# A fused LoRA kernel whose first load of 128 rows is issued as four transfers of 16, 16, 32 and 64 rows

## The chip, the cores and the metric

The kernel runs on one core of one Trainium2 chip. The metric is the device time of one execution in microseconds. Where a median is given, it is that of the runs shown beside it. All times in the profile are microseconds from the first instruction of the profiled execution.

## The reference

```python
def setup_inputs():
    batch, seq, d_model, r = 16, 512, 768, 16
    # x [16, 512, 768], A [768, 16], B [16, 768], float32; scale = 0.5

def reference(x, A, B, scale):
    lora = np.matmul(np.matmul(x, A), B)
    return (x + scale * lora).astype(np.float32)
```

The input x and the output have 8192 tokens of 768 float32 values, 25.17 MB each. A and B are 48 KB each.

## The kernel before

The 8192 tokens are 64 tiles of 128 tokens. `PARTS = [8, 8, 16, 16, 16]` groups them into five parts of x; in a part with S tiles partition p holds S tokens that follow one another in memory, so one partition reads or writes one contiguous run (`memory`, line 96). With S = 8 this run is 8 x 768 x 4 = 24,576 bytes. `x_all` holds 48 of the 64 tiles; the last part takes the room of the first two once these have been stored.

Seven loads (`LOADS`, line 106) and five stores (`STORES`, line 130) move x. All of them, and the small loads of A and B, are issued on SP's queue, in this order: the first load (line 140, ahead of the section in which the engines run their own programs), three loads of A as soon as POOL has cleared `a_rows` (line 163), B as soon as `b_rows` is cleared (line 167), four more loads of x (line 169), the first two stores (line 178, after the second group's first products), a load after each of these two stores has landed (lines 181 and 183), two stores, and the last store behind the section (line 361). Each load k has a semaphore of its own, `s_load[k]`, which counts 16 for a transfer.

The work goes in eight groups of eight tiles (`GROUP = 8`). For one group:

- ACT and POOL cast four tiles each to float16 into `xn` (`narrowed`, line 195, the copy on line 203). The first use of a load waits for its `s_load` (line 200).
- DVE transposes `xn` to `xt` in blocks of 32 (line 260); in the first group it does so in two halves (lines 271 to 274).
- PE multiplies by the block-diagonal weights `w_bd` into `y_ps`, 24 matmuls (line 290), ACT scales these into `y_bd` (line 245), and PE multiplies by `b_mm` into `lora` (line 311), two tiles at a time.
- DVE adds `lora` to x in place (line 265); when a part is finished, SP stores it.

DVE works one group behind the transposes: it transposes group g + 1 and then adds group g. PE's loop (line 333) interleaves in the same way. At the start, PE also waits for the weights: A is loaded, transposed by DVE (line 253) and spread by POOL (lines 220 to 229); B is loaded, cast by ACT (line 236), picked apart by PE (line 324) and cast again (line 238).

The first load is marked so that the planner adds no dependencies of its own to it (`no_tile_sem_insts`, and the group "first", which a no-op on POOL closes as a fence on line 144). The waits on `s_load[0]` in `narrowed` are the only ones for its data.

Of the kernel before, what the change touches and what calls it, by code (L numbers as in the profile page):

```python
# [28 lines left out]
def kernel(  # L29
# [8 lines left out]
    nc = tc.nc  # L38
    fp32 = mybir.dt.float32
    P = 128  # L40
# [3 lines left out]
    x2 = x.flatten_outer_dims()  # L44
# [38 lines left out]
    def sem(name):  # L83
        sems.append(nc.alloc_semaphore(name))
        return sems[-1]
# [10 lines left out]
    def memory(t2, i, s, n):  # L96
        S = PARTS[i]
        return t2[ds(parts[i], S * P), :].rearrange("(p s) d -> p s d", s=S)[:, ds(s, n), :]

    def held(i, s, n):  # L100
        return tiles(where.index((i, s)), n)

    def tiles(t, n):
        return x_all[:, ds(t % ROOM, n), :]

    LOADS = [
        (0, 0, 8), (1, 0, 8), (2, 0, 8), (2, 8, 8), (3, 0, 16), (4, 0, 8), (4, 8, 8)
    ]
    s_load = [sem(f"s_load{k}") for k in range(len(LOADS))]

    def load_of(t):
        i, s = where[t]
        return next(k for k, ld in enumerate(LOADS) if ld[0] == i and ld[1] <= s < ld[1] + ld[2])
# [20 lines left out]
    def load(k):  # L134
        ld = LOADS[k]
        return nc.sync.dma_start(out=held(*ld), in_=memory(x2, *ld)).then_inc(s_load[k], 16)

    first = load(0)  # L140
    tc.no_tile_sem_insts.add(first.ins.name)
    tc.add_to_no_dep_group("first", first.ins)
    begun = nc.gpsimd.nop()
    tc.declare_fence(begun.ins, group="first")

# [49 lines left out]
    def narrowed(e, copy, g, first, n=SUB):  # L195
        t = g * GROUP + first
        for k in dict.fromkeys(load_of(t + k) for k in range(n)):
            if (e, k) not in here:
                here.add((e, k))
                e.wait_ge(s_load[k], 16)  # L200
        if g:
            e.wait_ge(s_taken, g)
        ins = copy(out=xn[:, ds(first, n), :], in_=tiles(t, n))  # L203

        ins.then_inc(s_narrow if g else s_second if first else s_first, 1)

    def on_gpsimd(e):
        e.memset(a_rows[0:Q], 0.0).then_inc(s_ready, 1)  # L208
        e.memset(b_rows, 0.0).then_inc(s_brows, 1)  # L209
        e.memset(pick, 0.0).then_inc(s_pick, 1)  # L210
        e.memset(w_bd.rearrange("p c k m -> p (c k m)").bitcast(fp32), 0.0)  # L211
        e.memset(y_bd.rearrange("p s m -> p (s m)").bitcast(fp32), 0.0).then_inc(s_ready, 1)  # L212
        e.wait_ge(s_pick, 1)
        e.affine_select(  # L214
            out=pick, in_=pick, compare_op=mybir.AluOpType.not_equal, fill=1.0, base=0,
            pattern=[[0, NQ], [-APART, Q]], channel_multiplier=1,
        ).then_inc(s_pick, 1)
        narrowed(e, e.tensor_copy, 0, 0)
        e.wait_ge(s_ready, 3)
        e.tensor_copy(  # L220
            out=w_one.rearrange("i (c e) k r -> i c e (k r)", c=SETS),
            in_=a_t[0:Q].rearrange("i k r (e c) -> i c e (k r)", c=SET)[:, 0:SETS, 0:SET, :],
        ).then_inc(s_w, 1)
        e.wait_ge(s_w, 1)
        for b in range(NQ):
            e.tensor_copy(  # L226
                out=w_bd[ds(b * Q, Q), :, :, ds(b * Q, R)], in_=w_one
            ).then_inc(s_w, 1)
            e.wait_ge(s_w, b + 2)
        for g in range(1, NG):  # L230
            narrowed(e, e.tensor_copy, g, SUB)

    def on_scalar(e):
        narrowed(e, e.copy, 0, SUB)
        e.wait_ge(s_b, 16)
        e.copy(out=b_half, in_=b_rows).then_inc(s_bh, 1)  # L236
        e.wait_ge(s_bp, 1)
        e.copy(out=b_mm, in_=lora[0][:, 0, :]).then_inc(s_bm, 1)  # L238
        for g in range(NG):
            if g + 1 < NG:  # L240
                narrowed(e, e.copy, g + 1, 0)
            e.wait_ge(s_y, g + 1)
            for b in range(NQ):
                q = ds(b * Q, Q)
                last = e.mul(out=y_bd[q, :, q], in_=y_ps[q, :, :], mul=sc)  # L245
                if b == 0 and g + 1 < NG:

                    last.then_inc(s_narrow, 1)
            last.then_inc(s_spread, 1)
# [151 lines left out]
```

## Time and profile before

| | |
|---|---|
| median of 3 runs | 123.59 us (123.36 to 123.59) |
| profiled execution | 123.44 us |
| its span, first to last instruction | 121.7 us |
| DMA moved | 50.43 MB on one queue, mean 415 GB/s |
| DVE busy | 81.7 us (67% of the span) |
| PE, ACT, POOL busy | 50.0, 36.8, 28.8 us |
| granted TensorE clock, mean | 0.922 |

The page cuts the span into 40 slices of 3.04 us: a digit is the busy share in tenths. The row "DMA" is the mean busy share of the core's 16 DMA engines, "GB/s" what they moved. In a view of windows each row is a stretch of time, and its last columns are the granted clock, the DMA share and GB/s. In the chain of waits each row is a start, a duration and the engine or transfer that the end waited for. In the timeline each row is a start, a duration, the engine (SPq is SP's queue, and its time is that of the issue, not of the transfer), the line and the operation, and in brackets how long the engine was idle before, and what released it.

### The profile page before, as it was taken

Reading aid. Unit: us, or ns where it says so; the run is one execution under the profiler, and the core shown is the slowest. Engines: PE = TensorE matmul, PEld = TensorE weight load, DVE = VectorE, ACT = ScalarE, POOL = GpSimd, SP = SyncE. Lnnn points to the kernel's source line nnn. Section 1 sums busy time; section 2 is a strip of 40 time slices with the busy share of each in tenths; the row PEclk is TensorE's granted clock in tenths of the full one; section 3 lists DMA queues with packets and bytes.
Section 4 is the critical chain, followed back from the end, with each engine's and each line's share of the span. In section 5 each row is a group of like instructions: output and inputs, shape, how many; then the busy total and the mean of one; then the engine's idle time right before and its main releaser. Section 6 shows DMA issues by size and latency. Waiting matters only on the chain.

```text
span 121.7 us, 887 instructions
## 1 busy us (share of the span) xinstructions
PE 50.0 (41%) x322; PEld 29.2 (24%) x322; DVE 81.7 (67%) x42; ACT 36.8 (30%) x43; POOL 28.8 (24%) x23
## 2 busy tenths in 40 slices
PE   0000139477457547746745734774674420000000
PEld 0000016244233324424423312442442110000000
DVE  0002870699999999999999979999995991000000
ACT  4003728535408402835340193733004000000000
POOL 7603958035008002605300180620000000000000
PEclk9999999999999999999999999999999998555555
DMA  4999999999998897999999999998899899899890
GB/s 129 388 461 412 436 452 404 436 452 404 452 517 388 388 517 323 444 444 404 444 428 412 452 428 469 404 517 388 388 517 404 388 501 436 388 469 469 372 452 0
DMA packets 1784, 50.43 MB, mean 415 GB/s; under 512 B 220, under 2 KB 220, under 8 KB 248
## 3 DMA queue, kind: packets, MB, share of 16 engines
q1 hardware_dynamic: 1784, 50.43, 96.7%
HBM read 25.26 MB, written 25.17 MB: 414 GB/s over the span
## 4 chain that ended last, share of the span: by engine, by line
DVE 36%; DMA 29%; PE 9%; ACT 5%; POOL 2%; issue 1%
DVE x_sb L265 22%; DMA x_sb<-in_x_dram 20%; DVE xt L260 14%; DMA out_dram<-x_sb 9%; PE ps_yt L290 6%; PE lora_ps L311 3%; ACT y_bd L245 3%; POOL xn L203 2%; ACT xn L203 2%
## 5 line engine op out<-in xcount | busy, mean ns | idle before, releaser
L265 DVE TENSOR_TENSOR x_sb<-x_sb,lora_ps 128x1536 f32<-128x1536 f32 x32 | 53.7, 1734 | 1.4 <-PE lora_ps L311 1.4
L311 PE MATMUL lora_ps<-b_mm,y_bd 128*128 128x512 f16 (+1 forms) x128 | 25.0, 328 | 22.9 <-ACT y_bd L245 14.6
L203 POOL CAST xn<-x_sb 128x3072 f16<-128x3072 f32 x8 | 22.0, 2748 | 49.7 <-DMA x_sb<-in_x_dram 32.2
L203 ACT CAST xn<-x_sb 128x3072 f16<-128x3072 f32 x8 | 22.0, 2752 | 35.9 <-DMA x_sb<-in_x_dram 26.2
L260 DVE STREAM_TRANSPOSE xt<-xn 128x3072 f32<-128x3072 f32 (+1 forms) x9 | 27.0, 3007 | 6.3 <-ACT y_bd L245 5.8
L290 PE MATMUL ps_yt<-xt,w_bd 128*128 128x256 f16 x192 | 25.4, 283 | 10.8 <-DVE xt L260 10.8
L290 PEld LDWEIGHTS ps_yt<-xt,w_bd 128*128 128x128 f16 x192 | 18.6, 99 | 18.4 <-issue 14.0
L311 PEld LDWEIGHTS lora_ps<-b_mm,y_bd 128*128 128x128 f16 x128 | 10.5, 97 | 35.7 <-ACT y_bd L245 16.8
L245 ACT ACTIVATE y_bd<-ps_yt 32x256 f16<-32x256 f32 x32 | 12.0, 375 | 18.5 <-PE ps_yt L290 18.1
L253 DVE STREAM_TRANSPOSE a_t<-a_rows 32x1024 f32<-32x1024 f32 x1 | 2.0, 1964 | 11.4 <-DMA a_rows<-in_A_dram 11.4
L324 PE MATMUL lora_ps<-b_half,pick 128*128 128x512 f16 (+1 forms) x2 | 0.8, 500 | 14.7 <-ACT b_half L236 14.7
L324 PEld LDWEIGHTS lora_ps<-b_half,pick 128*128 128x128 f16 x2 | 0.1, 105 | 14.7 <-issue 14.7
L226 POOL COPY w_bd<-w_one 32x384 f16<-32x384 f16 x4 | 2.0, 501 | 0.2
L203 ACT ACT_TABLE_LOAD x1 | 1.3, 1283 | 1.0 <-POOLq L147 1.0
L211 POOL MEMSET w_bd<- 128x1536 f32 x1 | 1.4, 1372 | 0.0
L238 ACT CAST b_mm<-lora_ps 128x768 f16<-128x768 f32 x1 | 0.8, 799 | 1.0 <-PE lora_ps L324 1.0
L208 POOL MEMSET a_rows<- 32x1024 f32 x1 | 0.9, 942 | 0.6 <-POOLq L147 0.6
L220 POOL CAST w_one<-a_t 32x384 f16<-32x384 f32 x1 | 0.8, 843 | 0.0
L236 ACT CAST b_half<-b_rows 128x768 f16<-128x768 f32 x1 | 0.8, 826 | 0.0
L209 POOL MEMSET b_rows<- 128x768 f32 x1 | 0.7, 727 | 0.0
L212 POOL MEMSET y_bd<- 128x512 f32 x1 | 0.5, 515 | 0.0
L214 POOL TENSOR_SCALAR_AFFINE_SELECT pick<-pick 128x128 f16<-128x128 f16 x1 | 0.3, 300 | 0.0
(5 smaller groups left out, 0.6 us busy)
## 6 DMA issues: line engine op xcount, KB each, us to landing
x_sb<-in_x_dram SPq DMA_DIRECT2D x6, 3072.0 KB, 14.5
out_dram<-x_sb SPq DMA_DIRECT2D x3, 6144.0 KB, 19.3
x_sb<-in_x_dram SPq DMA_DIRECT2D x1, 6144.0 KB, 41.5
out_dram<-x_sb SPq DMA_DIRECT2D x2, 3072.0 KB, 14.2
a_rows<-in_A_dram SPq DMA_DIRECT2D x3, 16.0 KB
b_rows<-in_B_dram SPq DMA_DIRECT2D x1, 48.0 KB, 7.5
```

What stands on the lines that cost most here:

```text
L203: ins = copy(out=xn[:, ds(first, n), :], in_=tiles(t, n))
L208: e.memset(a_rows[0:Q], 0.0).then_inc(s_ready, 1)
L211: e.memset(w_bd.rearrange("p c k m -> p (c k m)").bitcast(fp32), 0.0)
L220: e.tensor_copy(out=w_one.rearrange("i (c e) k r -> i c e (k r)", c=SETS), in_=a_t[0:Q].rearrange("i k r (e c) -> i c e (k r)", c=SET)[:, ...
L226: e.tensor_copy(out=w_bd[ds(b * Q, Q), :, :, ds(b * Q, R)], in_=w_one).then_inc(s_w, 1)
L245: last = e.mul(out=y_bd[q, :, q], in_=y_ps[q, :, :], mul=sc)
L253: e.transpose(out=a_t[0:Q].rearrange("i k r c -> i (k r) c"), in_=a_rows[0:Q].rearrange("c (i k r) -> c (k r) i", k=2, r=R),).then_inc(s_r ...
L260: return e.transpose(out=ts[0], in_=ts[1])
L265: ins = e.tensor_tensor(out=xs, in0=xs, in1=lora[p % 2], op=mybir.AluOpType.add)
L290: mm = e.matmul(y_ps, w_bd[:, c, k, :], xv[:, :, c, :, k], start=(m == 0), stop=(m == MMS - 1),)
L311: mms.append(e.matmul(t[:, k, ds(n0, w)], y_bd[:, 2 * p + k, :], b_mm[:, ds(n0, w)], start=True, stop=True,))
L324: last = e.matmul(lora[0][:, 0, ds(n0, w)], pick.rearrange("p b r -> p (b r)"), b_half[:, ds(n0, w)], start=True, stop=True,)
```

## The change

The single issue of the first load is replaced by four, on the same queue and the same semaphore. `to[p:P:step]` takes every `step`-th partition from `p` on: partitions 0, 8, ..., 120 (16 rows), then 4, 12, ..., 124 (16 rows), then 2, 6, ..., 126 (32 rows), then the odd ones (64 rows). The four together move the same 128 rows, each row from and to the same place. The wait for load 0 is raised from 16 to 64. All other loads, stores and instructions stay as they are, on every engine, and in the same order.

```diff
-    first = load(0)
-    tc.no_tile_sem_insts.add(first.ins.name)
-    tc.add_to_no_dep_group("first", first.ins)
+    PIECES = [(0, 8), (4, 8), (2, 4), (1, 2)]
+    to, of = held(*LOADS[0]), memory(x2, *LOADS[0])
+    for p, step in PIECES:
+        piece = nc.sync.dma_start(out=to[p:P:step], in_=of[p:P:step]).then_inc(s_load[0], 16)
+        tc.no_tile_sem_insts.add(piece.ins.name)
+        tc.add_to_no_dep_group("first", piece.ins)
     begun = nc.gpsimd.nop()
     tc.declare_fence(begun.ins, group="first")
...
-                e.wait_ge(s_load[k], 16)
+                e.wait_ge(s_load[k], 16 if k else 16 * len(PIECES))
```

## The prediction

> **What bounds the kernel now.** I read the page's slices and queue rows first, then the chain of waits in order of time, then windows around the first load.
>
> ```profile
> PE 50.0 (41%) x322; PEld 29.2 (24%) x322; DVE 81.7 (67%) x42; ACT 36.8 (30%) x43; POOL 28.8 (24%) x23
> ...
> DMA  4999999999998897999999999998899899899890
> ...
> DMA packets 1784, 50.43 MB, mean 415 GB/s; under 512 B 220, under 2 KB 220, under 8 KB 248
> ...
> q1 hardware_dynamic: 1784, 50.43, 96.7%
> ```
>
> The DMA engines are full in nearly every slice but the first and the last, and DVE, the busiest compute engine, has 67%. So the time is a start, 50.43 MB at the full rate, and an end. All packets of 8 KB or more are 1784 - 248 = 1536 = 12 x 128: each of the seven loads and five stores of x moves one packet per partition, 24,576 bytes in the first load.
>
> ```profile
> 4.00:9.00 5.00, 0.00 (x0) 0.00 (x0) 0.00 (x0) 0.00 (x0) 0.91 (x3) 1.00 1.01 433
> 32.00:44.00 12.00, 7.15 (x48) 4.25 (x48) 12.00 (x7) 5.06 (x8) 2.75 (x1) 1.00 1.01 434
> 100.00:118.00 18.00, 0.00 (x0) 0.00 (x0) 0.85 (x1) 0.00 (x0) 0.00 (x0) 0.58 1.00 434
> ```
>
> The last two columns are the DMA share and GB/s. Loads alone (4 to 9 and 32 to 44 us) and stores alone (100 to 118) run at the same 433 to 434 GB/s with a share of 1.00 to 1.01. That is 433 / 16 = 27.1 GB/s for one of 16 engines, and 24,576 B / 27.1 GB/s = 0.91 us for one row. The first load is 8 rows per engine, 3.146 MB / 433 = 7.26 us.
>
> ```profile
> 0.74 10.35 DMA x_sb<-in_x_dram
> 11.09 0.05 issue
> 11.14 2.75 POOL xn L203
> ...
> 44.30 10.73 DMA out_dram<-x_sb
> 55.04 0.02 issue
> 55.05 14.55 DMA x_sb<-in_x_dram
> ```
>
> The chain begins with the load that is changed: issued at 0.74, landed 10.35 us later, which is 3.09 us more than 7.26. Whatever moves its end moves both the DMA queue behind it and the compute chain from 11.14 to the first store at 44.30, by about the same amount; the end follows one for one.
>
> **The start of the load.** The view of the DMA queue for 1 to 4 us, in 40 slices of 0.075 us (bytes are put down at the start of a packet):
>
> ```profile
> DMA  0000000000990999009797070070000999990709
> GB/s 0 0 0 0 0 0 0 0 0 0 983 655 0 655 328 328 0 0 328 328 655 328 0 328 0 0 328 0 0 0 0 655 655 983 655 655 0 328 0 655
> DMA packets 30, 0.74 MB, mean 246 GB/s; under 512 B 0, under 2 KB 0, under 8 KB 0
> ```
>
> A slice of 328 GB/s is one row begun (24,576 B / 0.075 us). Three begin at 1.75 us, and counting on, the sixteenth begins in the slice at 2.95; the next row begins only at 3.33, 1.58 us after the first three although a row takes 0.91. So the engines begin over 1.2 us, and the early ones are slow at first. Of the 0.74 MB begun by 4.00, half a row per engine (0.20 MB) is still to come: 0.54 MB done, which at 433 GB/s is a full flow begun at 4.00 - 1.25 = 2.75 us.
>
> **The change part by part.** *The engine's share of bytes* stays: 16, 16, 32 and 64 rows give each engine 1, 1, 2 and 4 rows if each piece spreads over all 16, the same eight. Each piece adds a completion on every engine, three more; in the next view 42 packets under 512 B pass with no fall of the rate, so nothing is taken for them.
>
> *Three more issues on SP.* From the timeline:
>
> ```profile
> 0.74 0.38 SPq L136 DMA_DIRECT2D x_sb<-in_x_dram  x1
> ...
> 1.06 0.94 POOL L208 MEMSET a_rows<- 32x1024 f32 x1 [0.62 <-POOLq L147]
> ...
> 2.03 2.01 SPq L163 DMA_DIRECT2D a_rows<-in_A_dram  x3
> ...
> 4.09 0.54 SPq L167 DMA_DIRECT2D b_rows<-in_B_dram  x1
> ...
> 4.68 2.07 SPq L136 DMA_DIRECT2D x_sb<-in_x_dram  x4
> ```
>
> One issue costs 0.38 us here, up to 2.01 / 3 = 0.67 later. Four pieces end at 0.74 + 4 x 0.38 = 2.3 to 0.74 + 4 x 0.67 = 3.4 instead of 1.12. The loads of A wait for a memset on POOL till 2.0 anyway, so they move from 2.03 by 0.3 to 1.4 us, and B and the four loads of x behind them end by 6.75 + 1.4 = 8.15. All of these queue behind the first load, whose 7.26 us from 2.75 last to 10.0: hidden with 1.8 us to spare. If that cover were gone, it would cost up to 1.4 us. Nor does the queue run dry between pieces: a piece comes every 0.38 to 0.67 us and keeps an engine busy for at least 0.91.
>
> *The start.* Sixteen rows instead of 128 have to be handed out before every engine has work. What this brings isn't in the trace: at best all engines flow fully from 1.75, a gain of 2.75 - 1.75 = 1.0 us; at worst the early slowness belongs to the first access and nothing is gained. Nothing is nearer to one end, so I take half, 0.5.
>
> *Which rows move together.* This decides the sign. The trace has the constant 27.1 GB/s per engine for 128-row transfers alone. It may be the limit of the engine, or of the part of SBUF that the row goes to, several partitions sharing one part. In the first case the pieces run at full rate: cost 0. In the second, a 128-row transfer runs undisturbed only because its rows are laid out so that no two engines go to one part at once. The pieces take partitions 0, 8, 16, ..., then 4, 12, ...: at one time all engines take rows of one kind, every second group of four partitions is left alone, and if the engines' numbers follow the rows, two engines share each part in every step: half rate, a cost of one more 7.26 us. What the trace has of narrow strided transfers is A and B (4 and 16 rows of 3 or 4 KB each):
>
> ```profile
> DMA packets 84, 0.46 MB, mean 464 GB/s; under 512 B 42, under 2 KB 42, under 8 KB 69
> ```
>
> From 9.7 to 10.7 us the 69 - 42 = 27 small data packets pass with no fall (464 GB/s). It speaks for the first case, but 27 packets of 4 KB are 0.1 MB, too short to fill whatever buffers lie between. Equal rates for reading and for writing HBM say that the limit is in the engine or on SBUF's side, and no more. I take the second case: the only shape shown at full rate is the one the change gives up, and the bursts against it are too small to count. From 7.26 something comes off: if two partners are d apart, the later is still in the old part for d while the earlier has moved on, and the rows make six stretches in one part (1, 1, 1, 1, 2, 2 rows), so 6d. With 1.2 us of spread cut to an eighth (16 rows for 128), d is about 0.1: 0.6 off. Ends: d = 0 (7.26), and d = 0.45, half a row (7.26 - 2.7 = 4.6).
>
> [...]
>
> **The sum.** The profiled execution took 123.44 us, 1.7 outside its span of 121.7; the median of the runs shown is 123.59, 0.15 above. Cost 7.26 - 0.6 for sharing, gain 0.5 at the start: +6.2, so 123.44 + 6.2 = 129.6.
>
> What is late next: the first store's issue moves from 44.30 to 50.5, and must still come before the loads run out.
>
> ```profile
> 47.80 2.75 ACT L203 CAST xn<-x_sb 128x3072 f16<-128x3072 f32 x1 [5.05 <-DMA x_sb<-in_x_dram]
> ```
>
> The fifth load of x lands at 47.8, so the store's issue is 3.5 us ahead of that; both move by about the same, and only an unequal move above 3.5 would leave a hole.
>
> **The rivals.**
> *Part of SBUF shared only in the first two pieces* (the layout of 32 and 64 rows keeps engines apart, as that of 128 does). Two rows at half rate cost 2 x 0.91 = 1.8, less 0.5: +1.3, 124.8 us; from 124.2 (gain 1.0, d = 0) to 125.3 (no gain). For it: the 128-row layout plainly keeps engines apart. Against: those pieces step over partitions.
> *The engine is the limit* (the other side). Nothing collides, the start's 0.5 is gained: 122.9, from 122.4 to 123.2. It decides once the sharing costs less than the gain of 0.5 us at the start. For it: the small packets of A and B lose nothing; against: only their size.
> *The change does not do what it says*: the early slowness is of the first access, not of handing out 128 rows, and nothing collides: 123.4 within 0.2. For it: the three rows that begin at 1.75 get nothing done before 3.3; against: engines that begin late, at 2.5 to 3.0, are not slow.
>
> **How the numbers follow.** Sharing throughout 0.46, its own range 123.44 + 4.6 - 1.0 = 127.0 to 123.44 + 7.26 = 130.7; sharing in two pieces 0.18; engine as limit 0.25; nothing 0.11. The likeliest gives 129.6. To leave out under 2 in 10 the range must take in most of the faster case: 122.6 to 130.7. Faster by over 0.2% (0.25 us, about what a measurement of this kernel can tell) 0.25, within it 0.11, slower 0.46 + 0.18 = 0.64.
>
> **What would show it.** Sharing: in the windows from 2 to 16 us the share stays near 1.0 and GB/s falls to some 220 to 300, the first cast of xn comes at 16 to 18 us instead of 11.1, and after it the rate is 433 again, every later step moved by the same amount. Two pieces only: low GB/s from 2 to 5.5 alone, cast at about 12.4. Engine as limit: sixteen rows begun by about 2.1 us, 433 GB/s from there, cast at about 10.6. Wrong in all of them: a cast moved with an end that doesn't follow, a hole in the DMA share at 45 to 55 us, or SP's issues of the later loads coming after the queue is empty.

## The result

| | median | runs |
|---|---|---|
| before | 123.37 us | 6 (123.27 to 123.59) |
| changed | 125.27 us | 6 (124.91 to 126.02) |

The ratio is 1.0153, with a 95% interval of 1.0123 to 1.0184: 1.9 us slower. The profiled execution took 125.39 us, 1.95 more than that of before, with a span of 123.6. One execution further down, 128.01 us with the widest piece first, fell into a slower state and is left out of its kernel's median.

The chain of waits of the changed kernel (start, duration, what the end waited for):

```profile
0.74 0.59 SPq L146
...
2.64 9.96 DMA x_sb<-in_x_dram
12.60 0.05 issue
12.65 2.75 POOL xn L209
...
46.69 9.84 DMA out_dram<-x_sb
56.53 0.01 issue
56.55 15.32 DMA x_sb<-in_x_dram
```

The first load lands at 12.60 instead of 11.09, 1.5 us later; the first store is issued at 46.69 instead of 44.30. Of these 2.4 us, 0.9 belong to the first 24 products on PE, 5.29 us instead of 4.41; a second execution of the kernel before had 5.05 there and its first store at 44.89, in the same total time.

Where the DMA engines lost it stands in the windows, here with the DMA share and GB/s as the last two columns, first before, then changed:

```profile
1.00:2.00 1.00, 0.00 (x0) 0.00 (x0) 0.00 (x0) 1.00 (x1) 0.94 (x2) 1.00 0.73 147
2.00:7.00 5.00, 0.00 (x0) 0.00 (x0) 0.00 (x0) 0.26 (x1) 2.91 (x6) 1.00 0.88 364
7.00:14.00 7.00, 0.00 (x0) 0.00 (x0) 2.04 (x2) 2.89 (x2) 2.86 (x2) 1.00 1.02 435
14.00:60.00 46.00, 28.00 (x179) 16.68 (x180) 41.01 (x21) 21.16 (x23) 16.42 (x10) 1.00 1.00 431
60.00:66.00 6.00, 2.93 (x22) 1.74 (x21) 6.00 (x4) 1.50 (x4) 0.00 (x0) 1.00 1.00 426
66.00:119.00 53.00, 19.04 (x126) 10.82 (x123) 32.70 (x18) 10.01 (x14) 5.50 (x2) 0.85 1.01 434
```

```profile
1.00:2.00 1.00, 0.00 (x0) 0.00 (x0) 0.00 (x0) 1.00 (x1) 0.93 (x2) 1.00 0.00 0
2.00:7.00 5.00, 0.00 (x0) 0.00 (x0) 0.00 (x0) 0.26 (x1) 2.91 (x6) 1.00 0.99 256
7.00:14.00 7.00, 0.00 (x0) 0.00 (x0) 1.21 (x1) 1.38 (x1) 1.35 (x1) 1.00 1.03 435
14.00:60.00 46.00, 27.34 (x169) 16.28 (x170) 39.46 (x21) 21.47 (x24) 16.70 (x11) 1.00 1.00 431
60.00:66.00 6.00, 3.52 (x25) 2.06 (x23) 6.00 (x4) 2.67 (x5) 1.20 (x1) 1.00 1.01 406
66.00:119.00 53.00, 21.72 (x132) 12.14 (x129) 35.08 (x19) 9.99 (x14) 5.49 (x2) 0.79 1.01 435
```

Turned into time at 433 GB/s: from 1 to 2 us 0.147 MB are missing (0.34 us), from 2 to 7 us 5 x 108 = 540 KB (1.25 us), from 60 to 66 us 6 x 20 = 120 KB (0.28 us), and elsewhere next to nothing. The sum is 1.87 of the 1.95 us. A row is booked whole at its start, so a window can be off by a row per engine, 0.39 MB or 0.9 us. The bytes begun since the start of the execution check it: 5.01 MB by 14 us before and 4.33 changed, which is 1.57 us behind; by 74 us 30.89 and 29.93, 2.2 us behind. From 2 to 7 us the engines are fuller than before (0.99 against 0.88) and move less: their packets are slow, not missing. From 7 us on the rate is 435, though most of the first load, the pieces of 32 and 64 rows, is still under way.

The queue from 1 to 4 us in slices of 0.075 us, as shown of before:

```profile
DMA  0000000000000099990809999000000099909009
GB/s 0 0 0 0 0 0 0 0 0 0 0 0 0 0 328 655 1311 983 0 328 0 328 328 655 328 0 0 0 0 0 0 0 328 655 328 0 655 0 0 328
```

The first row begins at 2.05 to 2.12 us instead of 1.75, and the sixteenth by 2.88.

### The profile page after: what moved, and what is told of

Same layout as the page of the kernel before. It is cut to its first block, busy times and chain, and to the rows that moved or that the text cites. A ratio compares the mean times of both kernels' runs of the same rounds, so it can differ in the third digit from the quotient of the medians.

```text
span 123.6 us, 890 instructions
## 1 busy us (share of the span) xinstructions
PE 52.6 (43%) x322; PEld 30.5 (25%) x322; DVE 81.8 (66%) x42; ACT 36.8 (30%) x43; POOL 28.8 (23%) x23
## 4 chain that ended last, share of the span: by engine, by line
DVE 35%; DMA 28%; PE 10%; ACT 5%; POOL 2%; SPq 1%; issue 1%
DVE x_sb L271 22%; DMA x_sb<-in_x_dram 20%; DVE xt L266 14%; DMA out_dram<-x_sb 8%; PE ps_yt L296 6%; PE lora_ps L317 3%; ACT y_bd L251 3%; POOL xn L209 2%; ACT xn L209 2%; SPq L146 1%
## 5 line engine op out<-in xcount | busy, mean ns | idle before, releaser
L317 PE MATMUL lora_ps<-b_mm,y_bd 128*128 128x512 f16 (+1 forms) x128 | 26.7, 344 | 22.3 <-ACT y_bd L251 14.4
L296 PE MATMUL ps_yt<-xt,w_bd 128*128 128x256 f16 x192 | 26.6, 292 | 10.0 <-DVE xt L266 10.0
L296 PEld LDWEIGHTS ps_yt<-xt,w_bd 128*128 128x128 f16 x192 | 19.3, 103 | 18.0 <-issue 13.1
L317 PEld LDWEIGHTS lora_ps<-b_mm,y_bd 128*128 128x128 f16 x128 | 11.1, 101 | 35.8 <-ACT y_bd L251 16.8
```

The source lines that it names most:

```text
L296: mm = e.matmul(y_ps, w_bd[:, c, k, :], xv[:, :, c, :, k], start=(m == 0), stop=(m == MMS - 1),)
L317: mms.append(e.matmul(t[:, k, ds(n0, w)], y_bd[:, 2 * p + k, :], b_mm[:, ds(n0, w)], start=True, stop=True,))
```

## The experiments

Each was timed against the kernel before on the same chip, with 123.38 or 123.39 us as its median. Edits are against the changed kernel unless said otherwise. Where an expectation speaks of 1.70 us, it is the time that one row of the second piece takes; the starts of the rows give the same, about 4.0 us for the middle one of the second piece's sixteen and 5.7 for that of the next sixteen.

### Two pieces of 64 rows

```diff
-    PIECES = [(0, 8), (4, 8), (2, 4), (1, 2)]
+    PIECES = [(0, 2), (1, 2)]
```

> The first load as two transfers of 64 rows (even partitions, then odd). In the changed kernel the rows of the first three steps are slow (1.70 us in the second piece) and all rows of the 64-row piece take 0.91. Theory 'places': 16 rows reach only half of the places in SBUF, while 64 rows are laid out with one place per engine; no row beyond the first is slow here, the time is 123.4 plus at most 0.4 for a later start: 123.3 to 123.8. Theory 'source': rows two apart in memory are not far enough apart to collide: the same. Theory 'start' (whatever comes first is slow, by 1.5 us more as soon as the first load is several transfers): 124.5 to 125.3.

Measured: 123.72 us, ratio 1.003 (1.0018 to 1.0043). The queue from 1 to 4 us:

```profile
DMA  0000000000000099999000000000000000077999
GB/s 0 0 0 0 0 0 0 0 0 0 0 0 0 0 655 1638 655 1966 328 0 0 0 0 0 0 0 0 0 0 0 0 0 0 0 0 328 328 983 983 983
```

All sixteen first rows begin within five slices, 0.38 us instead of 1.2, so the rows are handed out as fast as could be wished. But they begin at 2.05 us, and no second row begins before 3.6, 1.5 us later. The slowness of the first rows is not a matter of handing out 128 rows.

### Four pieces of 32 rows

```diff
+    PIECES = [(0, 4), (1, 4), (2, 4), (3, 4)]
```

> The first load as four transfers of 32 rows, every fourth. As many transfers, issues and completions as in the changed kernel, but no piece of 16 rows. Theory 'places': 32 rows reach all places; rows at 0.91 us after the first, time 123.4 plus the later start: 123.4 to 124.0. Theory 'number of transfers' (each issue or completion costs): 125 to 125.5, as the changed kernel. Theory 'source' (rows 4 x 24,576 bytes apart collide half as much as 8 x): 124.0 to 124.8. If 32 rows were laid out by blocks so that engines share places, all eight rows would be slow: about 129.

Measured: 123.69 us, ratio 1.0034 (1.0021 to 1.0047), with as many transfers, issues and completions as the changed kernel. Its window:

```profile
2.00:7.00 5.00, 0.00 (x0) 0.00 (x0) 0.00 (x0) 0.26 (x1) 2.92 (x6) 1.00 1.05 393
```

393 GB/s against 256 in the changed kernel and 364 before. The number of transfers costs nothing that shows beside the 0.3 us that two pieces of 64 rows cost as well, and pieces of 32 rows run at about the full rate (408 GB/s from 4 to 9 us, before 433). The first load even landed at 10.95 us, 0.14 earlier than before, and the kernel is still no faster: the landing alone does not set the end.

### Eight pieces of 16 rows

```diff
+    PIECES = [(p, 8) for p in range(8)]
```

> The first load as eight transfers of 16 rows, every eighth partition. Theories 'places' and 'source': every row of the load is slow (1.70 instead of 0.91 us): 8 x 0.79 = 6.3 us more, less the half microsecond that the first row loses anyway: 128.8 to 130. Theory 'start': only the first three rows are slow: 125 to 126.

Measured: 130.95 us, ratio 1.0619 (1.0601 to 1.0636): 7.57 us more, above the expected range. The row of the queue for 5 to 17 us:

```profile
DMA packets 212, 2.46 MB, mean 205 GB/s; under 512 B 106, under 2 KB 106, under 8 KB 113
...
q1 hardware_dynamic: 212, 2.46, 98.0%
```

Full engines (98%) at 205 GB/s, a little under half of 433, for as long as the pieces last. A whole load at half rate is 7.26 us more, and 0.3 us of later start makes 7.6; at the 205 GB/s of this window the load would take 8.1 us more, so the agreement is good to half a microsecond only. So 16 rows are slow at any time, not in the beginning alone.

### The same places, read in order

```diff
+    at = 0
...
-        piece = nc.sync.dma_start(out=to[p:P:step], in_=of[p:P:step]).then_inc(s_load[0], 16)
+        rows = P // step
+        piece = nc.sync.dma_start(out=to[p:P:step], in_=of[at : at + rows]).then_inc(s_load[0], 16)
...
+        at += rows
```

> The four pieces of the changed kernel go to the same partitions, but each is read from rows that follow one another in memory, so the rows of the first load are in another order (the output's rows of the first part with them). Theory 'places' (the SBUF side decides): nothing changes against the changed kernel: 125 to 125.6, second rows at 1.70. Theory 'source' (rows 196,608 bytes apart in HBM collide): the loss goes, 123.4 to 123.9.

Measured: 125.17 us, ratio 1.0151 (1.0132 to 1.017), as the changed kernel (125.27). This kernel leaves out the order of the rows in the first part, so its output there is not the reference's; shapes, bytes and instructions are the same. Its windows differ in shape (315 GB/s from 2 to 7 us and 407 from 7 to 14, where the changed kernel has 256 and 435), but by 14 us it has begun 4.42 MB against 4.33. Where the rows lie in HBM didn't matter for the time here. That leaves the side that is written, SBUF, and the next experiment changes that side alone.

### Pieces of neighbouring rows

```diff
-    PIECES = [(0, 8), (4, 8), (2, 4), (1, 2)]
+    PIECES = [(0, 16), (16, 16), (32, 32), (64, 64)]
...
-    for p, step in PIECES:
-        piece = nc.sync.dma_start(out=to[p:P:step], in_=of[p:P:step]).then_inc(s_load[0], 16)
+    for p, n in PIECES:
+        piece = nc.sync.dma_start(out=to[p : p + n], in_=of[p : p + n]).then_inc(s_load[0], 16)
```

> The same sizes of piece as in the changed kernel, but of neighbouring rows: 0 to 15, 16 to 31, 32 to 63, 64 to 127, so each is read in order and written in order. Theory 'places', several neighbouring partitions sharing one: neighbouring rows reach fewer places than rows spread by eight, so that the load is slower still than in the changed kernel: above 129, and if a row of the first piece takes four times 0.91 and all others at least twice, 123.4 + 0.3 + 2 x 2.7 + 6 x 0.91 = 134.6. Theory 'spread rows cost' (what is slow is the step between the partitions): 123.4 to 124. [...]

Measured: 133.66 us, ratio 1.0832 (1.0817 to 1.0848): 10.3 us more, where the arithmetic with quarter and half rates had 11.2. It reads the same rows in the same pieces as the experiment before it, and differs only in the partitions that are written: 8.5 us for that alone. So it isn't the step between partitions that makes these transfers slow; which partitions the rows go to decides, as it would if few places were shared, though no run shows a place by itself. The queue from 1 to 4 us, windows, and SP's timeline:

```profile
GB/s 0 0 0 0 0 0 0 0 0 0 1966 1311 328 1311 328 0 0 0 0 0 0 0 0 0 0 0 0 0 0 0 0 0 0 0 0 0 0 328 328 0
```

```profile
2.00:7.00 5.00, 0.00 (x0) 0.00 (x0) 0.00 (x0) 0.26 (x1) 2.91 (x6) 1.00 0.81 98
...
13.00:14.00 1.00, 0.00 (x0) 0.00 (x0) 0.00 (x0) 0.00 (x0) 0.00 (x0) 1.00 1.92 393
14.00:15.00 1.00, 0.00 (x0) 0.00 (x0) 0.00 (x0) 0.00 (x0) 0.00 (x0) 1.00 0.00 0
```

```profile
0.74 1.91 SPq L146 DMA_DIRECT2D x_sb<-in_x_dram  x4
```

The sixteen first rows begin at 1.75 us, without delay, and four issues take 1.91 us, 0.48 each with their gaps. The 98 GB/s from 2 to 7 us are too low, as most first rows are booked ahead of 2 us. The starts of the rows say more: the middle one of the second piece begins at about 4.2 us and that of the third at 7.65, so a row takes 3.4 us, 116 GB/s for sixteen, 3.7 times the 0.91 us of the 128-row load. The four times 0.91 us of the expectation was the author's assumption; it stands there for the first piece, whose rows took some 2.4 us, from about 1.85 to the same 4.2.

The 64 neighbouring rows at the end have four rows per engine, which begin at 12.0, 13.75, 15.7 and 17.6 us: 1.75 to 1.95 us for a row, the half rate that pieces of 16 spread rows have. That speaks against a rival for those, that a transfer of one row per engine is slow as such. It is not excluded by itself, since no run has a piece of sixteen rows that ran at the full rate.

### The widest piece first

```diff
+    PIECES = [(1, 2), (2, 4), (4, 8), (0, 8)]
```

> The four pieces of the changed kernel in the reverse order: 64, 32, 16, 16 rows. Theory 'places': the two pieces of 16 rows are as slow at the end of the load as at its beginning, 2 x 0.91 = 1.8 us, and the later start of 0.3 us (as with two of 64 rows) stays: 123.4 + 2.1 = 125.5, somewhat above the changed kernel, if the slow first access hid part of its first piece. Theory 'start' (narrow pieces are slow only while the first accesses are): 123.7.

Measured: 126.35 us (126.11 to 126.96), ratio 1.0228 (1.021 to 1.0245), 0.85 us above what 'places' gave and 2.65 above 'start'. Three windows of the profiled execution, 126.96 us:

```profile
2.00:7.00 5.00, 0.00 (x0) 0.00 (x0) 0.00 (x0) 0.26 (x1) 2.91 (x6) 1.00 1.04 388
7.00:14.00 7.00, 0.00 (x0) 0.00 (x0) 0.66 (x1) 0.63 (x1) 0.60 (x1) 1.00 0.99 302
...
60.00:66.00 6.00, 3.47 (x25) 1.90 (x23) 6.00 (x5) 3.42 (x5) 1.94 (x1) 1.00 0.97 348
```

The wide pieces run well, the narrow ones behind them are slow: from 7 to 14 us 7 x 133 KB are missing, 2.15 us, against a gain of 0.28 from 2 to 7 us and a loss of 0.34 from 1 to 2 us. That makes 2.2, as 'places' had it. The rest, 6 x 78 KB or 1.08 us, was lost between 60 and 66 us, which neither theory knew.

### Two pieces of half rows

```diff
-    PIECES = [(0, 8), (4, 8), (2, 4), (1, 2)]
+    PIECES = [0, 4]
...
-    for p, step in PIECES:
-        piece = nc.sync.dma_start(out=to[p:P:step], in_=of[p:P:step]).then_inc(s_load[0], 16)
+    for s in PIECES:
+        piece = nc.sync.dma_start(out=to[:, ds(s, 4), :], in_=of[:, ds(s, 4), :]).then_inc(s_load[0], 16)
```

> The first load as two transfers of all 128 rows, half of each row (12,288 bytes) at a time. It asks where the later start of about 0.35 us comes from that two of 64 and four of 32 rows show (first packet at 2.10 instead of 1.76, issue 0.58 instead of 0.38). If it is the step between the partitions or the number of rows: first issue 0.38, first packet at 1.76, time 123.2 to 123.5. If it is that another transfer follows: 123.6 to 123.8, first packet at 2.1.

Measured: 123.42 us, ratio 1.0 (0.9991 to 1.0009), no difference. SP's timeline and the queue from 1 to 4 us:

```profile
0.74 0.85 SPq L146 DMA_DIRECT2D x_sb<-in_x_dram  x2
```

```profile
GB/s 0 0 0 0 0 0 0 0 0 164 819 328 655 164 0 164 164 0 0 0 0 0 164 164 492 328 655 328 164 0 492 164 655 819 0 164 328 492 655 819
```

Two issues in 0.85 us with the gap between them, and the first packet at 1.7 us. So a second transfer doesn't delay the first. Together with the pieces of neighbouring rows, which also begin at 1.75, it leaves the step between partitions as what the late ones share: with a step of 2 (two of 64 rows), 4 or 8 the first packet comes at 2.05 to 2.1 us, and four issues take 2.49 us in the changed kernel against 1.91 without a step. The step on SBUF's side is enough: read in order, the first packet comes at 2.05 too.

### A in one transfer

This is the kernel before with A loaded in another way.

```diff
-        for c in range(SETS):
-            e.dma_start(
-                out=a_rows[c : SET * SET : SET, :], in_=blocks[ds(c * SET, SET), :]
-            ).then_inc(s_a, 16)
+        e.dma_start(out=a_rows[0:NC, :], in_=blocks).then_inc(s_a, 16)
...
```

DVE's wait for A and the order in which the weights are cast are changed to match.

> The kernel before, with A loaded in one transfer of 12 rows instead of three of 4 (and the cast of the weights reading its blocks in that order). It takes the load's row view at its word: the last DMA engine ends later than most, in the changed kernel and before, and three transfers of 4 rows give few engines three packets each of 4,096 bytes (0.16 us at the rate of 27.1 GB/s). If those engines set the end: 0.2 to 0.35 us less, 123.05 to 123.2. If the end is set by who starts last: no change, 123.4.

Measured: 124.17 us, ratio 1.0065 (1.0042 to 1.0089), slower, which neither theory had. From 7 to 14 us it moved 414 GB/s, before 435, and from 60 to 66 us 352, before 426:

```profile
7.00:14.00 7.00, 0.00 (x0) 0.00 (x0) 1.97 (x1) 2.63 (x1) 2.60 (x1) 1.00 1.02 414
...
60.00:66.00 6.00, 3.60 (x24) 2.12 (x24) 6.00 (x3) 1.50 (x4) 0.00 (x0) 1.00 0.96 352
```

Here too the new transfer puts rows in neighbouring partitions (0 to 11) where the old ones went four partitions apart. That this is why the 7 to 14 us are slower fits the rest, but wasn't tried by itself. Something else moved with it: SP saves two issues, so that B is issued at 2.71 us instead of 4.09 and the next loads of x from 3.32 instead of 4.68, and their rows can meet those of the first load earlier. No run tells the two apart.

### The spread of the changed kernel

The changed kernel twice more, the widest piece first once more, and the kernel before once more, one execution each.

> The changed kernel once more. Its profile shows two losses: 1.6 us by 7 us (1 to 7 us: fewer bytes moved), and 0.28 us between 60 and 66 us, where the first two stores end and the sixth load of x begins (406 against 426 GB/s). If the second is what its executions differ by (124.91 to 126.02), then the rate from 1 to 7 us is the same again and time minus 125.0 goes with the loss in a window of 6 us around the end of the second store. If the start differs, then the rate from 2 to 7 us is other than 256 GB/s by more than 15.

> The changed kernel, a further execution, to see its spread: the same two readings as for r1_after, 256 GB/s within 15 from 2 to 7 us if the start is always alike, and the rest of the difference around 60 to 66 us.

> The pieces in reverse order once more. It was 3.3 us slower than before where 2.1 was expected, and lost 1.08 us between 60 and 66 us (348 against 426 GB/s). If that later loss is of this execution alone, it and the time fall together, to as little as 125.5; if it belongs to the order of the pieces, 126.1 or more with a loss near 1 us again.

> The kernel before once more, to see whether the window from 60 to 66 us is as undisturbed in another execution: 426 GB/s within 10, time 123.2 to 123.6. If the later loss comes and goes in this kernel too, it says nothing of the change.

The last two columns are the bytes begun since the start of the execution.

| | us | 2 to 7 us | 60 to 66 us | by 14 us | by 74 us |
|---|---|---|---|---|---|
| changed, first | 125.39 | 256 GB/s | 406 GB/s | 4.33 MB | 29.93 MB |
| changed, second | 125.30 | 256 | 406 | 4.35 | 29.93 |
| changed, third | 125.94 | 275 | 422 | 4.33 | 29.98 |
| widest first, first | 126.96 | 388 | 348 | 4.06 | 29.52 |
| widest first, second | 126.05 | 393 | 369 | 4.10 | 29.64 |
| before, first | 123.44 | 364 | 426 | 5.01 | 30.89 |
| before, second | 123.41 | 354 | 414 | 5.06 | 30.77 |

The kernel before moved 12 GB/s less from 60 to 66 us in its second execution, in the same time, so a difference of that size says nothing. With the widest piece first, a loss of 0.8 us is there again, and the time is near the 126.1 that was expected for that.

The expectation for the changed kernel fell: neither stretch tells the slowest execution from the others. It has the better windows from 2 to 7 and from 60 to 66 us, but by 14 us it has moved as much as they have, and by 74 us not less. What it has that the other two lack is a hole behind that. Its windows and SP's timeline, and SP's timeline of the first execution:

```profile
76.00:77.00 1.00, 0.03 (x1) 0.03 (x2) 1.00 (x1) 0.90 (x3) 0.00 (x0) 1.00 0.92 393
77.00:78.00 1.00, 1.00 (x7) 0.61 (x8) 1.00 (x1) 0.00 (x0) 0.00 (x0) 1.00 0.29 123
```

```profile
77.39 9.02 SPq L164 DMA_DIRECT2D out_dram<-x_sb  x2
```

```profile
76.91 8.62 SPq L164 DMA_DIRECT2D out_dram<-x_sb  x2
```

Few rows begin from 77 to 78 us: the last loads have been handed out, and the third store was issued only at 77.39. One such window may deceive, as a row is booked at its start. Counted from the starts, with 0.91 us for each row, the engines that have a row under way fall to 3 to 5 of 16 between 77.8 and 78.2 us, an estimate; in the other two executions the third store's rows come in time, at 12 of 16. The first execution with the widest piece first, whose third store was issued at 78.62, has such a hole too, at 79.0 to 79.4 us. Before:

```profile
74.42 8.83 SPq L158 DMA_DIRECT2D out_dram<-x_sb  x2
...
76.93 2.75 ACT L203 CAST xn<-x_sb 128x3072 f16<-128x3072 f32 x1 [2.98 <-DMA x_sb<-in_x_dram]
```

There the store came at 74.42, 2.5 us ahead of the last load's landing. In the changed kernel's first profile it came at 76.91, 2.49 us later, while the first load had moved by 1.5: the sixth load is issued when the first store has landed, and then passes the slow stretch after 60 us. The cover is nearly used up, and in the third execution it was gone. There the sixth load landed at 72.58 us instead of 71.87, and the third store came 0.5 us later for it; why it landed later, though as many bytes had been begun by 74 us, the traces don't show.

## Why the prediction was wrong

It had the direction and the side that costs, SBUF's, and a size more than three times too large: +6.2 us against +1.9.

- *What bounds the kernel*: right. In the windows of both kernels the rate is 431 to 435 GB/s wherever it is not disturbed, and the windows have nearly the whole loss in two stretches of the queue.
- *Same bytes, three more completions, three more issues*: right. Four pieces of 32 rows have all of these and run at full rate. SP's four issues took 2.49 us, within 4 x 0.38 to 4 x 0.67, hidden as reckoned.
- *The start, a gain of 0.5 us between 0 and 1.0*: wrong in sign, by about 0.8 us. The bounds left out a loss, which none of the rows excluded. The rows were handed out faster (0.38 instead of 1.2 us with two pieces of 64), as the step said, but that wasn't what the early rows waited for, and a step between partitions put the first packet off by 0.3 us. Two pieces of 64 and four of 32 show this part without the narrow pieces, 0.3 us in the whole time.
- *Which rows move together*: the step that failed. The prediction's choice, SBUF's side, is what the runs point to: reading in order changed nothing (125.17 us), and with the same reading other partitions changed everything (133.66). That several partitions share a part of SBUF, counted in groups of four, was the author's assumption; the runs show rates by partitions alone, 408 GB/s with every fourth (4 to 9 us, pieces of 32) and 205 with every eighth (5 to 17 us, pieces of 16). What failed is "if the engines' numbers follow the rows, two engines share each part in every step", by which all eight rows of an engine were to be slow, 7.26 us. That fits 16 rows only. Spread pieces of 32 and 64 rows run as if laid out without sharing (+0.3 us for the whole load), so two rows in eight are slow, which cost 1.25 us by 7 us. How rows are dealt to engines isn't seen directly. The price itself was about right: with every row in a piece of 16 it is 7.57 us, 7.26 and the later start. No run shows the stretches in one part from which the 0.6 for partners that are apart was counted, and nothing was off that sum.
- *The rival with two slow pieces* had 124.8 us, from 124.2 to 125.3, and is what happened, at 125.27. Its 1.8 us for two rows is seen where the narrow pieces come last (2.15 us from 7 to 14 us, less the 0.28 gained before). Where they come first, only 1.25 us are missing from 2 to 7 us, since the first row is slow in any case: 1.2 to 1.6 us with two pieces of 64 rows too. The later start of 0.34 and the 0.28 us after 60 us make up the rest. So its pattern held, narrow pieces at about half rate (205 GB/s) and wide ones at the full (435 from 7 to 14 us), while the time lies in its range partly by luck: a cheaper pair of rows and two losses that it didn't have nearly cancel. Its argument against, that the pieces step over partitions, counted for nothing: the evidence for it stood in the constant rate of the 128-row transfers (433 to 434 GB/s).
- *The end follows one for one*: nearly. The landing moved by 1.51 us and the end by 1.95, through the later stretch after 60 us, and in one execution through a hole at 77 to 78 us as well. The cover of the first store was named; that of the third, 2.5 us, was not, and it is the one that ran out.

What stays open is why the stretch from 60 to 66 us, where the second store ends and the sixth load begins, moves 348 to 426 GB/s in one kernel or another. It was slower in the kernels whose first microseconds were changed in some ways, but not with four pieces of 32 rows or with half rows (426 in both), and not in step with the time of each execution. The windows' edges blur it; by the bytes begun, the distance to the kernel before grew from 54 to 74 us by 0.7 to 0.9 us with the widest piece first and with A in one transfer, by 0.4 to 0.5 in the changed kernel, and by 0.3 in the second execution of the kernel before. No run takes it by itself.

No version tried here beats the kernel before; two pieces of half rows equal it.

## What to carry to other kernels

How fast a transfer of few rows ran depended here on the partitions that they go to. Against 433 GB/s for 128 rows, 16 rows ran at about half rate even when spread over all of SBUF (205 GB/s), 16 neighbouring ones at about a quarter (116, the second such piece), 64 neighbouring ones at half (1.75 to 1.95 us for a row instead of 0.91), and 32 or 64 spread ones at about the full rate (393 and 388 GB/s from 2 to 7 us, where the kernel before has 364). Before splitting a load to start sooner, see whether its first rows wait for being handed out or for the first access; here, with two pieces of 64 rows, all sixteen were begun within 0.4 us and still took 1.5. And where a queue is always full, look at each issue's lead over the queue's end: here a loss of 1.5 us at the start became 2.5 at the third store's issue, whose lead had been 2.5.

## What the runs showed of the hardware

- A step between partitions put off a load's first packet: 2.05 to 2.1 us with steps of 2, 4 or 8, 1.7 to 1.75 without, from an issue at 0.74, and an issue took longer (four in 2.49 us with the steps of the changed kernel against 1.91 with neighbouring rows).
- The first row of each engine took 1.2 to 1.6 us instead of 0.91 when sixteen began together: two pieces of 64 rows, begun at 2.05 to 2.43, have their second rows from 3.6 on, and pieces of 16 spread rows, begun from 2.05, from 3.4 on. Sixteen neighbouring rows took longer, from 1.75 to 3.8.
- Which partitions a load writes decided 8.5 us between two kernels that read the same rows in the same pieces (125.17 and 133.66 us).
- A stretch in which stores give way to a load lost 0.8 to 1.1 us from 60 to 66 us with the widest piece first (348 and 369 GB/s) and with A in one transfer (352), 0.28 in two executions of the changed kernel (406; 422 in a third), and nothing with four pieces of 32 rows or half rows (426, as before), with a DMA share of 0.96 to 1.04.
